# Instance norm over 512 channels: a small early write to the output, moved behind the first unit's sum

## The chip, the cores and the metric

The kernel runs on one core of a Trainium2 chip. The metric is the device time of one execution, in microseconds (us). A profile is one execution recorded by the hardware profiler; its span runs from the core's first to its last instruction. PE is TensorE, DVE is VectorE, ACT is ScalarE, POOL is GpSimd, SP is SyncE; ACTq, SPq and POOLq are the instruction queues from which DMAs are issued.

## What is computed

`x` has the shape (4, 8, 16, 256, 256) in float32, `gamma` the shape (8, 16). Each of the 4 x 8 x 16 = 512 channels is normalised over its own 256 x 256 = 65,536 values and scaled:

```
mu = x.mean(axis=(3, 4), keepdims=True)
var = ((x - mu) ** 2).mean(axis=(3, 4), keepdims=True)
out = (x - mu) / np.sqrt(var + 1e-5) * gamma[None, :, :, None, None]
```

134.2 MB are read and as many written.

## The kernel before

**Tiling.** The 512 channels are cut into 32 units of 16 channels. A unit is a tile of 128 partitions by 8,192 float32 values (4.19 MB, 4,096 KB in the profile): a channel lies on 8 neighbouring partitions. Six slots `xt` (AHEAD = 6) hold units in SBUF; unit u uses slot u mod 6. A unit is read once, changed in place and written back from its slot.

**One unit** (the loop over u, lines 103 to 134). VectorE sums each partition's row (L105); ScalarE sums the squares of the same row (L106, its elementwise result thrown away in `junk`); TensorE multiplies both sums with a small constant matrix, which adds the 8 partitions of a channel (L114); VectorE and ScalarE make the variance, the root, the reciprocal and the scale (L115, L119, L123, L125); VectorE applies shift and scale to the tile in place (L128). The store of the unit is issued from ScalarE's queue (L132), and the load of unit u + 6 into the same slot, which has to wait until that store has landed, from SP's queue (L48).

**Before the loop.** The loads of units 0 to 5 are issued at once, units 1 and 3 from ScalarE's queue, the others from SP's. GpSimd loads gamma into `g_row` (L55) and builds the constant matrix `navg` (L65 to L70); VectorE spreads gamma (`g_rep`, L81), TensorE turns it into a column (L86), VectorE copies that to `g_col` (L92), which L125 reads first for unit 0.

**The touch.** `touch` is a tile of 16 partitions by 128 float32 values. VectorE fills it with zeros (L53), and GpSimd's first DMA (L54) writes it to the first 512 bytes of every eighth row of unit 0 of `out`: 16 pieces of 512 bytes. Unit 0's store overwrites them later, so the result does not depend on them. Both write the same bytes, so the store of unit 0 waits on its queue until the touch has landed.

**What sets the order.** The kernel declares a manual schedule: every engine runs its instructions in the order in which the program names them. An engine's queue is strictly in order: an instruction that waits holds up all that stand behind it on that engine, issues of DMAs included. On ScalarE's queue the square of unit u + 1 stands behind the store of unit u. On GpSimd's queue nothing stands behind the building of `navg`.

Of the kernel before, what the change touches and what calls it, by code (L numbers as in the profile page):

```python
# [1 line left out]

# [4 lines left out]

F32 = mybir.dt.float32
U8 = mybir.dt.uint8
ALU = mybir.AluOpType  # L10
ACTF = mybir.ActivationFunctionType
AX = mybir.AxisListType


@with_exitstack
def kernel(
    ctx: ExitStack,
    tc: tile.TileContext,
    x: bass.AP,
    gamma: bass.AP,  # L20
    out: bass.AP,
):
    nc = tc.nc
    B, G, C, H, W = x.shape
    P = nc.NUM_PARTITIONS
    HW = H * W
    n_ch = B * G * C
    S = 8
    K = P // S
    F = HW // S  # L30
    U = n_ch // K
    NG = (G * C) // K
    AHEAD = 6
    assert HW % S == 0 and (G * C) % K == 0

    xv = x.rearrange("b g c h w -> (b g c h w)").rearrange("(u p f) -> u p f", p=P, f=F)
    ov = out.rearrange("b g c h w -> (b g c h w)").rearrange("(u p f) -> u p f", p=P, f=F)
    gv = gamma.rearrange("g c -> (g c)")

    data = ctx.enter_context(tc.tile_pool(name="data", bufs=1))  # L40
    singles = ctx.enter_context(tc.tile_pool(name="singles", bufs=1))
    psum = ctx.enter_context(tc.tile_pool(name="psum", bufs=4, space=bass.MemoryType.PSUM))
    ctx.enter_context(tc.manual_schedule())

    slots = [data.tile([P, F], F32, name=f"xt{i}") for i in range(AHEAD)]

    def load(u, queue):
        queue.dma_start(out=slots[u % AHEAD][:], in_=xv[u])  # L48


    g_row = singles.tile([1, G * C], F32, name="g_row")
    touch = singles.tile([16, 128], F32, name="touch")
    nc.vector.memset(touch[:], 0.0)  # L53
    nc.gpsimd.dma_start(out=ov[0][0::S, 0:128], in_=touch[:])  # L54
    nc.gpsimd.dma_start(out=g_row[:], in_=gv[None, :])  # L55
    for u in range(AHEAD):
        load(u, nc.scalar if u in (1, 3) else nc.sync)


    eps_t = singles.tile([P, 1], F32, name="eps_t")  # L60
    nc.gpsimd.memset(eps_t[:], 1e-5)
    one = singles.tile([1, 1], F32, name="one")
    nc.gpsimd.memset(one[:], 1.0)
    navg = singles.tile([P, K, S], F32, name="navg")
    nc.gpsimd.memset(navg[:], -1.0 / HW)  # L65
    nc.gpsimd.affine_select(  # L66
        out=navg[:], in_=navg[:], pattern=[[-S, K], [0, S]], compare_op=ALU.is_ge,
        fill=0.0, base=0, channel_multiplier=1,
    )
    nc.gpsimd.affine_select(  # L70
        out=navg[:], in_=navg[:], pattern=[[S, K], [0, S]], compare_op=ALU.is_ge,
        fill=0.0, base=S - 1, channel_multiplier=-1,
    )
    navg_w = navg[:].rearrange("p k s -> p (k s)")
    root_eps = singles.tile([P, 1], F32, name="root_eps")
    nc.scalar.activation(out=root_eps[:], in_=eps_t[:], func=ACTF.Sqrt)  # L76
    g_rep = singles.tile([1, NG, K, S], F32, name="g_rep")
    g_ps = psum.tile([P, NG], F32, name="g_ps", bufs=1)
    g_col = singles.tile([P, NG], F32, name="g_col")

    nc.vector.tensor_copy(  # L81
        out=g_rep[:],
        in_=g_row[:].rearrange("o (n k) -> o n k", n=NG).unsqueeze(3).to_broadcast([1, NG, K, S]),
    )
    for n in range(NG):
        nc.tensor.matmul(  # L86
            out=g_ps[:, n : n + 1],
            lhsT=g_rep[:, n].rearrange("o k s -> o (k s)"),
            rhs=one[:],
            start=True, stop=True,  # L90
        )
    nc.vector.tensor_copy(out=g_col[:], in_=g_ps[:])  # L92

    junk = singles.tile([P, F], U8, name="junk")

    st = singles.tile([P, U, 2], F32, name="st")
    nvar = singles.tile([P, U], F32, name="nvar")
    std = singles.tile([P, U], F32, name="std")
    rstd = singles.tile([P, U], F32, name="rstd")
    scale = singles.tile([P, U], F32, name="scale")  # L100

    squares = []
    for u in range(U):
        t = slots[u % AHEAD]
        nc.vector.reduce_sum(out=st[:, u, 0:1], in_=t[:], axis=AX.X)  # L105
        square = nc.scalar.activation(  # L106
            out=junk[:], in_=t[:], func=ACTF.Square, accum_out=st[:, u, 1:2],
        )
        if u:

            tc.declare_no_dep(square.ins, squares[-1].ins, reason="junk, ordered by the root between")
        squares.append(square)
        ps = psum.tile([P, 2], F32, name="ps")
        nc.tensor.matmul(out=ps[:], lhsT=navg_w, rhs=st[:, u], start=True, stop=True)  # L114
        nc.vector.tensor_scalar(  # L115
            out=nvar[:, u : u + 1], in0=ps[:, 0:1], scalar1=ps[:, 0:1],
            scalar2=ps[:, 1:2], op0=ALU.mult, op1=ALU.add,
        )
        nc.scalar.activation(  # L119
            out=std[:, u : u + 1], in_=nvar[:, u : u + 1], func=ACTF.Sqrt,  # L120
            bias=eps_t[:], scale=-1.0,
        )
        nc.vector.reciprocal(out=rstd[:, u : u + 1], in_=std[:, u : u + 1])  # L123
        g = u % NG
        nc.vector.tensor_mul(  # L125
            out=scale[:, u : u + 1], in0=rstd[:, u : u + 1], in1=g_col[:, g : g + 1],
        )
        nc.vector.tensor_scalar(  # L128
            out=t[:], in0=t[:], scalar1=ps[:, 0:1], scalar2=scale[:, u : u + 1],
            op0=ALU.add, op1=ALU.mult,  # L130
        )
        nc.scalar.dma_start(out=ov[u], in_=t[:])  # L132
        if u + AHEAD < U:
            load(u + AHEAD, nc.sync)


# [1 line left out]
_INS = ['x', 'gamma']  # L138
_OUTS = [((4, 8, 16, 256, 256), 'float32')]


# [23 lines left out]
```

## Time and profile before

| | before |
|---|---|
| median of 3 runs | 627.45 us (626.88 to 627.5) |
| span of the profiled execution | 625.4 us (its whole time is not listed) |
| busy: VectorE, ScalarE, PE, POOL | 443.4, 238.8, 21.4, 2.4 us |
| moved by DMA | 268.46 MB, 429 GB/s over the span |
| packets of queue q10 (issues of ACT) | 142.61 MB, 52.9% of the 16 DMA engines' span |
| packets of queue q1 (issues of SP) | 125.83 MB, 46.7% |
| packets of queue q0 (issues of POOL) | 0.01 MB, 0.0% |

Busy times are shares of the work of each engine and say little here by themselves. The page gives the DMA engines' rate in 40 equal slices of the span; the chain that ended last follows the last instruction back to what released it; a group's row gives the busy time, the mean duration and the idle time ahead of it with what ended it; a row of DMA issues gives the time from the issue to the landing; the table of stretches gives busy times and rates between two points of time, counted from the start of the span.

### The profile page before, as it was taken

To read this page: it belongs to the slowest core of one execution; us is meant where nothing else is said; L and a number is where in the kernel's file an instruction comes from. 1 tells how busy PE (TensorE), PEld (TensorE's weight loads), DVE (VectorE), ACT (ScalarE), POOL (GpSimd) and SP (SyncE) were. 2 spreads that over 40 slices of the span, in tenths; PEclk is the share of its full clock that TensorE was granted. 3 is DMA by queue.
4 is the path that set the end of the run, shared out by engine and by line. 5 is a ranking of instruction groups with operands and counts; after the bars stand their busy time and mean duration, and the time that the engine had idled before them with its cause. 6 is when DMAs were issued, how large, how long until landed. Compare 5 with 4: busy or idle time off the path is not lost.

```text
span 625.4 us, 631 instructions
## 1 busy us (share of the span) xinstructions
PE 21.4 (3%) x80; PEld 19.5 (3%) x80; DVE 443.4 (71%) x163; ACT 238.8 (38%) x98; POOL 2.4 (0%) x11
## 2 busy tenths in 40 slices
PE   0200000000000000000000000000000000000000
PEld 0200000000000000000000000000000000000000
DVE  0588999999776687666776767867668676686730
ACT  0444444444443244432344423444224442244400
POOL 1000000000000000000000000000000000000000
DMA  8999999999999999999999999999999999999998
GB/s 369 436 402 436 436 436 436 436 434 424 434 436 432 432 428 434 436 436 436 436 434 423 434 436 432 436 428 434 434 436 436 436 436 432 425 434 434 434 432 363
DMA packets 9282, 268.46 MB, mean 429 GB/s; under 512 B 1072, under 2 KB 1088, under 8 KB 1088
## 3 DMA queue, kind: packets, MB, share of 16 engines
q10 hardware_dynamic: 4896, 142.61, 52.9%
q1 hardware_dynamic: 4320, 125.83, 46.7%
q0 software_dynamic: 64, 0.01, 0.0%
q14 instruction: 2, 0.02, 0.0%
HBM read 134.22 MB, written 134.23 MB: 429 GB/s over the span
## 4 chain that ended last, share of the span: by engine, by line
another core or an unknown queue 61%; DMA 17%; DVE 15%; SPq 1%; PE 1%; issue 0%; ACT 0%
DVE st L105 10%; DMA xt<-in_x_dram 10%; DMA out_dram<-xt 8%; DVE xt L128 5%; SPq L48 1%; PE ps L114 1%; ACT std L119 0%; DVE nvar L115 0%; DVE rstd L123 0%; DVE scale L125 0%
## 5 line engine op out<-in xcount | busy, mean ns | idle before, releaser
L105 DVE TENSOR_REDUCE st<-xt 128x1 f32<-128x8192 f32 x32 | 277.9, 8685 | 100.8 <-DMA xt<-in_x_dram 100.8
L106 ACT ACTIVATE junk<-xt 128x8192 uint8<-128x8192 f32 x32 | 225.0, 7030 | 275.6 <-DMA xt<-in_x_dram 232.4
L128 DVE TENSOR_SCALAR xt<-xt,ps,scale 128x8192 f32<-128x8192 f32 x32 | 145.6, 4551 | 1.2
L119 ACT ACTIVATE std<-nvar,eps_t 128x1 f32<-128x1 f32 x32 | 9.4, 295 | 79.6 <-DVE nvar L115 79.6
L114 PE MATMUL ps<-st,navg 128*128 128x2 f32 x64 | 17.8, 348 | 557.6 <-DVE st L105 557.6
L114 PEld LDWEIGHTS ps<-st,navg 128*128 128x128 f32 x64 | 16.0, 311 | 559.4 <-issue 559.4
L115 DVE TENSOR_SCALAR nvar<-ps 128x1 f32<-128x1 f32 x32 | 9.2, 288 | 23.8 <-PE ps L114 23.8
L123 DVE RECIPROCAL rstd<-std 128x1 f32<-128x1 f32 x32 | 5.3, 164 | 11.6 <-ACT std L119 11.6
L81 DVE COPY g_rep<-g_row 1x1024 f32<-1x1024 f32 x1 | 0.7, 681 | 14.2 <-DMA g_row<-in_gamma_dram 14.2
L106 ACT ACTIVATION_READ_ACCUMULATOR junk<-xt 128x1 f32 x32 | 6.0, 187 | 0.0
L125 DVE TENSOR_TENSOR scale<-rstd,g_col 128x1 f32<-128x1 f32 x32 | 5.1, 160 | 1.1
L86 PE MATMUL g_ps<-one,g_rep 1*128 1x1 f32 x16 | 3.5, 347 | 16.1 <-DVE g_rep L81 16.1
L86 PEld LDWEIGHTS g_ps<-one,g_rep 1*128 1x128 f32 x16 | 3.5, 326 | 16.1 <-issue 16.1
L92 DVE COPY g_col<-g_ps 128x8 f32<-128x8 f32 x1 | 0.2, 167 | 3.7 <-PE g_ps L86 3.7
L76 ACT ACT_TABLE_LOAD x1 | 1.3, 1283 | 1.7 <-PEq L149 1.7
L53 DVE MEMSET touch<- 16x128 f32 x1 | 0.2, 165 | 0.9 <-PEq L149 0.9
L54 POOL DMA_DIRECT2D out_dram<-touch x1 | 0.6, 617 | 0.8 <-DVE touch L53 0.8
L55 POOL DMA_DIRECT2D g_row<-in_gamma_dram x1 | 0.5, 484 | 0.0
L66 POOL TENSOR_SCALAR_AFFINE_SELECT navg<-navg 128x128 f32<-128x128 f32 x1 | 0.4, 398 | 0.1
L70 POOL TENSOR_SCALAR_AFFINE_SELECT navg<-navg 128x128 f32<-128x128 f32 x1 | 0.4, 397 | 0.1
L65 POOL MEMSET navg<- 128x128 f32 x1 | 0.2, 231 | 0.0
L76 ACT ACTIVATE root_eps<-eps_t 128x1 f32<-128x1 f32 x1 | 0.2, 203 | 0.0
(6 smaller groups left out, 0.6 us busy)
## 6 DMA issues: line engine op xcount, KB each, us to landing
out_dram<-xt ACTq DMA_DIRECT2D x32, 4096.0 KB, 62.5
xt<-in_x_dram SPq DMA_DIRECT2D x30, 4096.0 KB, 38.5
xt<-in_x_dram ACTq DMA_DIRECT2D x2, 4096.0 KB, 31.7
out_dram<-touch POOLq DMA_DIRECT2D x1, 8.0 KB, 9.1
g_row<-in_gamma_dram POOLq DMA_DIRECT2D x1, 0.5 KB, 13.3
```

What stands on the lines that cost most here:

```text
L48: queue.dma_start(out=slots[u % AHEAD][:], in_=xv[u])
L76: nc.scalar.activation(out=root_eps[:], in_=eps_t[:], func=ACTF.Sqrt)
L81: nc.vector.tensor_copy(out=g_rep[:], in_=g_row[:].rearrange("o (n k) -> o n k", n=NG).unsqueeze(3).to_broadcast([1, NG, K, S]),)
L86: nc.tensor.matmul(out=g_ps[:, n : n + 1], lhsT=g_rep[:, n].rearrange("o k s -> o (k s)"), rhs=one[:], start=True, stop=True,)
L105: nc.vector.reduce_sum(out=st[:, u, 0:1], in_=t[:], axis=AX.X)
L106: square = nc.scalar.activation(out=junk[:], in_=t[:], func=ACTF.Square, accum_out=st[:, u, 1:2],)
L114: nc.tensor.matmul(out=ps[:], lhsT=navg_w, rhs=st[:, u], start=True, stop=True)
L115: nc.vector.tensor_scalar(out=nvar[:, u : u + 1], in0=ps[:, 0:1], scalar1=ps[:, 0:1], scalar2=ps[:, 1:2], op0=ALU.mult, op1=ALU.add,)
L119: nc.scalar.activation(out=std[:, u : u + 1], in_=nvar[:, u : u + 1], func=ACTF.Sqrt, bias=eps_t[:], scale=-1.0,)
L123: nc.vector.reciprocal(out=rstd[:, u : u + 1], in_=std[:, u : u + 1])
L125: nc.vector.tensor_mul(out=scale[:, u : u + 1], in0=rstd[:, u : u + 1], in1=g_col[:, g : g + 1],)
L128: nc.vector.tensor_scalar(out=t[:], in0=t[:], scalar1=ps[:, 0:1], scalar2=scale[:, u : u + 1], op0=ALU.add, op1=ALU.mult,)
```

## The change

The memset of `touch` and its DMA are no longer issued ahead of the gamma load but inside the loop, for unit 0 only, right after VectorE's first sum:

```diff
     g_row = singles.tile([1, G * C], F32, name="g_row")
     touch = singles.tile([16, 128], F32, name="touch")
-    nc.vector.memset(touch[:], 0.0)
-    nc.gpsimd.dma_start(out=ov[0][0::S, 0:128], in_=touch[:])
     nc.gpsimd.dma_start(out=g_row[:], in_=gv[None, :])
...
     for u in range(U):
         t = slots[u % AHEAD]
         nc.vector.reduce_sum(out=st[:, u, 0:1], in_=t[:], axis=AX.X)
+        if u == 0:
+
+            nc.vector.memset(touch[:], 0.0)
+            nc.gpsimd.dma_start(out=ov[0][0::S, 0:128], in_=touch[:])
         square = nc.scalar.activation(
```

The memset does not read the sum: it comes after it because VectorE runs in order. GpSimd's DMA waits for the memset. Its instruction now stands last on GpSimd's queue, behind the building of `navg`; the gamma load stands first there. The store of unit 0 waits for the touch as before.

## The prediction

> **What bounds the kernel now.** I read the bandwidth row of the page first, then the chain that ended last, then a table of stretches. In the page's row below each figure is the rate of one fortieth of the span (15.6 us).
>
> ```profile
> GB/s 369 436 402 436 436 436 436 436 434 424 434 436 432 432 428 434 436 436 436 436 434 423 434 436 432 436 428 434 434 436 436 436 436 432 425 434 434 434 432 363
> ```
>
> It is flat from the second slice to the thirty-ninth, whatever the engines do: VectorE is busy 71%, ScalarE 38%. Apart from its two ends only the third slice (31 to 47 us) is low, at 402. The chain of waits tells the same from the other side (start, duration, what):
>
> ```profile
> 112.28 0.02 issue
> 112.30 47.77 DMA out_dram<-xt
> ...
> 160.44 18.97 another core or an unknown queue
> ```
>
> Unit 5's store is issued at 112.3 and lands 47.8 us later, since other transfers stand ahead of it. From there each load waits in SP's queue for the store that frees its slot, about 19 us a time (the row says unknown queue; the waits of SP's own queue name the stores, 534.9 us in 26 waits). To see what a unit costs I took stretches of 19.36 us, the spacing of those waits. The columns are the stretch, its length, then PE, PEld, DVE, ACT and POOL busy, granted clock, DMA share, GB/s:
>
> ```profile
> 1.00:20.36 19.36, 3.54 (x16) 3.49 (x16) 0.90 (x3) 1.49 (x2) 2.18 (x7) 1.00 0.97 407
> 20.36:39.72 19.36, 0.56 (x2) 0.50 (x2) 15.97 (x6) 9.11 (x4) 0.00 (x0) 1.00 1.00 433
> 39.72:59.08 19.36, 0.56 (x2) 0.50 (x2) 18.18 (x6) 11.85 (x4) 0.00 (x0) 1.00 1.00 410
> 59.08:78.44 19.36, 1.12 (x4) 1.00 (x4) 17.01 (x10) 8.71 (x6) 0.00 (x0) 1.00 1.00 433
> ```
>
> Long stretches from 97.8 to 485 also give 433. One load and one store are 8.39 MB, and 8.39 MB at 433 GB/s is 19.37 us: **the transfers set the time**. 268.46 MB at 433 are 620.0 us of the 625.4. The stretch from 39.72, in which the first store starts, lost (433 - 410)/433 x 19.36 = 1.03 us, the first one (433 - 407)/433 x 19.36 = 1.16. So the change can cost only what makes the DMA engines idle or slow, and can gain little more than these two losses, 2.2 us.
>
> The span is 625.4 us; the profiled execution's whole time is not listed. The median 627.45 is 2.05 above the span, and I put my differences on the median.
>
> **The change, part by part.** The rows around the place where the touch goes (start, duration, engine, line, operation, idle time before it):
>
> ```profile
> 22.57 8.69 DVE L105 TENSOR_REDUCE st<-xt 128x1 f32<-128x8192 f32 x1 [2.71 <-DMA xt<-in_x_dram]
> ...
> 32.00 0.29 DVE L115 TENSOR_SCALAR nvar<-ps 128x1 f32<-128x1 f32 x1 [0.74 <-PE ps L114]
> ...
> 33.05 4.55 DVE L128 TENSOR_SCALAR xt<-xt,ps,scale 128x8192 f32<-128x8192 f32 x1
> ...
> 37.63 0.35 ACTq L132 DMA_DIRECT2D out_dram<-xt  x1
> 38.03 7.03 ACT L106 ACTIVATE junk<-xt 128x8192 uint8<-128x8192 f32 x1 [5.41 <-DVE xt L128]
> ```
>
> and the issues (KB each, us from issue to landing):
>
> ```profile
> out_dram<-touch POOLq DMA_DIRECT2D x1, 8.0 KB, 9.1
> g_row<-in_gamma_dram POOLq DMA_DIRECT2D x1, 0.5 KB, 13.3
> ```
>
> *Taken from the start.* One memset (L53, 0.165 us), POOL's 0.85 us wait for it and one issue (0.617 us). The gamma load, next on POOL's queue, starts at about 1.36 - 0.85 = 0.51 us instead of 1.98, and its row lands between 0.51 + 9.1 = 9.6 and 0.51 + 13.3 = 13.8 us, not at 15.29. g_rep, 16 small matmuls and g_col (done at 19.87) come earlier by as much. Their first reader is L125 at 32.85: 13 us of cover, worth nothing. SP and ACT issue their first loads at 0.81 as before. 8 KB less in the first stretch is 8192 B at 433 GB/s = 0.02 us. Gain 0.
>
> *The memset after the first sum.* L105 ends at 31.26; the memset takes 0.165 us in VectorE's idle 0.74 us before L115 (which waits for PE). Cost 0; without that cover, 0.165 us of VectorE.
>
> *POOL's issue.* It is now POOL's last instruction, so nothing stands behind it. Before, POOL began 0.30 us after the memset's end (1.06 to 1.36); now 31.43 + 0.30 = 31.73, ending at 32.35, ahead of L128. The landing time beside a busy VectorE and in midstream is not shown. Nearest row: its own, 9.1 us, with four loads queued then too; I take 40.8. Later by rows: g_row's 13.3 gives 45.0; if POOL's work were held until L128 ends at 37.60, 37.60 + 9.1 = 46.7; a load's 38.5 us (median), the far end, 70.2. Below nothing: alone in its queue it may land sooner, which gains nothing, because L128 ends at 37.60 anyway.
>
> VectorE's L128 sweeps its tile in 4.55 us, L105 one of the same size in 8.69. [...]
>
> *Store 0.* L132 on ACT's queue waits for the touch, since both write unit 0 of out: issued at 40.8 instead of 37.63. What does that cost? In ACT's queue stand loads 1 and 3 ahead of it. SP's and ACT's queues share evenly: loads 0 and 1 land 21.7 and 21.9 us after issue, 2 and 3, issued at 1.2, after 41.4 and 41.5, at 42.6. Store 0, issued at 37.63, lands after 24.9 us at 62.5, one period of 19.4 after that 42.6. So it lies idle for some 4 to 5 us now. An issue moves bytes within 1.2 us (issued at 0.81, 328 GB/s between 1.00 and 2.00): 40.8 + 1.2 = 42.0 is in time. Cost 0. If the touch is later, ACT's queue is empty, but SP's holds loads 4 and 5, due at 62.3 and 81.7, and they take the bandwidth. A lone queue of stores runs at 431 GB/s (596 to 616 us); a lone queue of loads no row shows. It lies between 433 and 339, the rate from 1 to 4 us, the start included.
>
> *Behind store 0 on ACT* is unit 1's square: 38.03 becomes 41.2, done with its accumulator read (0.19) at 48.4. PE waited for VectorE's sum at 46.2, now for this: unit 1 is 2.2 us late, and so are the units behind it up to unit 5, issued at 114.5. Its store had 47.8 us of other transfers ahead of it: cover enough. Store 1 (52.56 to 54.8) is still ahead of store 0's end. Cost 0.
>
> Sum: 0, **627.4 us**.
>
> **The rivals.**
> *B, the loss at the first store goes.* If the 1.03 us stands for a first write to out that the touch at 1.36 prepared too early, a touch just ahead cures it: 627.45 - 1.03 = 626.4. For it: no later store shows a dip of that size. Against: nothing shows that the touch works on it. With all of the start's loss too, 625.2.
> *C, a first write in midstream.* The touch went in while the first stretch was losing 1.16 us anyway; among full queues it may cost a loss of its own, as store 0 does: +1.03, 628.5; twice that (data, then completion), 629.5. Against: the stretch has ordinary reasons for its loss (no bytes before 1.00).
> *D, the touch is late (the slower side).* The mechanism: store 0 waits on ACT's queue for a touch that lands after about 41.4, and loads 4 and 5 alone keep the engines going. At 46.7 store 0 moves at 47.9, 5.3 us after 42.6; 5.3 x (1 - 339/433) = 1.15 us at most: 628.6. From 42.6 + 19.4 = 62.0 on, both queues are dry and each us costs one: a touch at 70.2 gives 71.4 - 62.0 = 9.4 us, 636.9. For it: every transfer of before beside full queues took 9 us or more. Against: 16 us lie between 46.7 and 62.
> *E, the change does not do what it says.* A scheduler could move the touch back; but the order is written by hand, and in the built kernel the memset stands right after sum 0 and the issue last on POOL: 2%.
>
> **How the numbers follow.** About 0.2% (1.25 us) is what a measurement of this kernel tells from no change. A, my forecast: 0.36, 627.2 to 627.7. B: 0.14, half over the bound. C: 0.22, 0.13 over it. D: 0.26, 0.24 over it, since a late touch would also bring C's loss into full queues (1.15 + 1.03 = 2.2). E: 0.02. Faster 0.07; slower 0.13 + 0.24 = 0.37; same 0.36 + 0.07 + 0.09 + 0.02 + 0.02 = 0.56. The range leaves out B's outer half (0.07) and D's long waits (about 0.10): 626.2 to 629.8 (627.45 + 2.2, rounded up).
>
> **What the profile after would show.** A: landing of the touch 9 to 10 us after an issue at 31.7, store 0's issue at about 40.8, the stretch from 39.72 at 410 again, 433 behind it. B: that stretch near 433. C: a second low stretch, around 36 to 41. D: POOL's issue longer than 0.62 us or a landing past 45, and less than 433 while SP's queue runs alone. I am wrong if the rate of the long middle changes, or the start before 2 us moves.

## The result and the profile after

The changed kernel takes **642.65 us** (median of 4 runs, 641.61 to 643.71) against 627.41 (median of 4, 626.88 to 627.5): a ratio of 1.0245, 95% interval 1.0232 to 1.0259. The prediction was 627.4 us with a range of 626.2 to 629.8. The change costs 15 us where I had counted nothing. The profiled execution has a span of 639.9 us and took 641.61. The granted clock is 1.00 in every run of this document.

I read the views in the same order as before. The bandwidth row of the changed kernel's page:

```profile
GB/s 381 438 394 434 434 406 428 418 434 422 426 426 422 422 428 424 430 430 426 432 426 418 428 420 434 426 426 426 430 426 426 428 422 430 420 424 436 430 434 213
```

Up to the fifth slice it looks as before. From the sixth (80 us) on, the plateau, 423 to 436 before, has gone down: 406 in the sixth, then 418 to 434, with 436 in one late slice; the last slice holds half a slice's bytes. The table of stretches, with the same columns as before (the last figure is GB/s), puts numbers on it:

```profile
1.00:20.36 19.36, 3.54 (x16) 3.48 (x16) 0.85 (x2) 1.49 (x2) 1.71 (x6) 1.00 0.97 406
20.36:39.72 19.36, 0.55 (x2) 0.50 (x2) 15.99 (x7) 7.42 (x3) 0.51 (x1) 1.00 1.01 434
39.72:59.08 19.36, 0.59 (x2) 0.50 (x2) 17.26 (x6) 12.51 (x4) 0.00 (x0) 1.00 1.00 408
59.08:78.44 19.36, 1.12 (x4) 1.00 (x4) 17.11 (x7) 9.74 (x6) 0.00 (x0) 1.00 1.00 428
...
97.80:291.40 193.60, 6.14 (x22) 5.51 (x22) 148.93 (x56) 81.58 (x33) 0.00 (x0) 1.00 1.00 425
291.40:485.00 193.60, 5.02 (x18) 4.50 (x18) 134.29 (x47) 72.88 (x28) 0.00 (x0) 1.00 1.00 427
...
620.00:639.90 19.90, 0.00 (x0) 0.00 (x0) 0.00 (x0) 0.00 (x0) 0.00 (x0) 1.00 0.60 257
```

The same two long stretches of the kernel before, and its last one:

```profile
97.80:291.40 193.60, 6.14 (x22) 5.52 (x22) 151.51 (x55) 81.54 (x33) 0.00 (x0) 1.00 1.00 433
291.40:485.00 193.60, 5.58 (x20) 5.01 (x20) 138.49 (x50) 74.19 (x30) 0.00 (x0) 1.00 1.00 433
...
616.00:625.40 9.40, 0.00 (x0) 0.00 (x0) 0.00 (x0) 0.00 (x0) 0.00 (x0) 1.00 0.73 314
```

The place where the touch goes in (20 to 40 us) is as fast as ever, and the stretch of the first store loses what it lost before (408 against 410). The loss lies in what follows. From 97.8 to 485 us, (433 - 425)/433 x 193.6 + (433 - 427)/433 x 193.6 = 6.3 us; from 59 to 98 us, at 428 twice, 0.4 us; from 485 to 580, at 426, 1.5 us. The tail of 19.9 us at 257 GB/s lacks (433 - 257)/433 x 19.9 = 8.1 us of full rate, before's tail 2.6: 5.5 us more. Together 13.7 of the 14.5 us by which the span grew. The DMA engines are called busy throughout (share 1.00) and move less.

The trace's packet records say how. A packet of 32,768 bytes takes 1.213 us of its engine (the median, before and after). Each engine moves 8 packets of a store and 8 of a load in a period, and before they take turns, one from ACT's queue, one from SP's (all 5,271 neighbouring pairs between 100 and 500 us). (The records do not name the engine; I put packets together by the end of one and the start of the next.) Between 60 and 580 us, 15 of 6,878 such packets took more than 1.26 us before, and 505 of 6,756 after, up to 2.2 us. Of the 505, 434 are loads, and about 300 of these stand in the two turns behind the end of a store on the same engine; in the first part, from 60 to 200 us, 135 of 140 do. Their excess is 8.7 us for each engine, close to the 8.2 us of the stretches. And the engines come apart: the first and the last engine's completion of one store lie 1.1 us apart before (unit 25), and 8.7 us after; in the tail the first engine has finished at 629.3 us and the last at 638.6.

The chain of waits has the same form, with a longer step: before, SP waited 18.97 us from load to load, now 19.0 to 20.1.

```profile
98.38 46.35 DMA out_dram<-xt
144.78 0.33 SPq L48
145.11 19.23 another core or an unknown queue
...
321.96 19.99 another core or an unknown queue
```

And the rows around the touch (start, duration, engine, line, operation, idle time before it), with the issues' rows:

```profile
31.33 0.17 DVE L106 MEMSET touch<- 16x128 f32 x1
...
31.80 0.51 POOL L107 DMA_DIRECT2D out_dram<-touch  x1 [28.63 <-DVE touch L106]
...
33.15 4.55 DVE L130 TENSOR_SCALAR xt<-xt,ps,scale 128x8192 f32<-128x8192 f32 x1
...
39.76 0.35 ACTq L134 DMA_DIRECT2D out_dram<-xt  x1
40.16 7.03 ACT L108 ACTIVATE junk<-xt 128x8192 uint8<-128x8192 f32 x1 [7.43 <-DMA out_dram<-touch]
...
62.30 0.56 PE L116 MATMUL ps<-st,navg 128*128 128x2 f32 x2 [14.38 <-DVE st L103]
```

```profile
g_row<-in_gamma_dram POOLq DMA_DIRECT2D x1, 0.5 KB, 9.2
out_dram<-touch POOLq DMA_DIRECT2D x1, 8.0 KB, 7.9
```

The memset hides behind PE, the touch is issued at 31.80 and lands at 31.80 + 7.88 = 39.68, and unit 0's store is issued at 39.76 in place of 37.63: 2.1 us late. By unit 2 PE waits for VectorE's sum again, at 62.30 where it did so at 61.27 before: the compute is 1.0 us late and gets no later. All of this is close to the prediction, and none of it explains 15 us by itself.

### The profile page after: what moved, and what is told of

Its sections match the earlier page's. It is cut to its first block, busy times and chain, and to the rows that moved or that the text cites. A ratio compares the mean times of both kernels' runs of the same rounds, so it can differ in the third digit from the quotient of the medians.

```text
span 639.9 us, 631 instructions
## 1 busy us (share of the span) xinstructions
PE 21.4 (3%) x80; PEld 19.5 (3%) x80; DVE 443.3 (69%) x163; ACT 238.8 (37%) x98; POOL 2.4 (0%) x11
## 4 chain that ended last, share of the span: by engine, by line
another core or an unknown queue 64%; DMA 14%; DVE 9%; issue 5%; ACT 1%; SPq 1%; PE 0%; POOL 0%; ACTq 0%; POOLq 0%
DMA out_dram<-xt 7%; DMA xt<-in_x_dram 6%; DVE st L103 5%; DVE xt L130 4%; DMA out_dram<-touch 1%; SPq L48 1%; ACT junk L108 1%; PE ps L116 0%; ACT std L121 0%; DVE nvar L117 0%; DVE rstd L125 0%; DVE scale L127 0%; POOL g_row L53 0%; POOL navg L64 0%
## 5 line engine op out<-in xcount | busy, mean ns | idle before, releaser
L130 DVE TENSOR_SCALAR xt<-xt,ps,scale 128x8192 f32<-128x8192 f32 x32 | 145.6, 4551 | 1.2
## 6 DMA issues: line engine op xcount, KB each, us to landing
xt<-in_x_dram SPq DMA_DIRECT2D x30, 4096.0 KB, 36.8
```

Of the source, the lines that this page charges most:

```text
L130: nc.vector.tensor_scalar(out=t[:], in0=t[:], scalar1=ps[:, 0:1], scalar2=scale[:, u : u + 1], op0=ALU.add, op1=ALU.mult,)
```

## The experiments

At first I had three theories. **P**: the late store misses its turn among the transfers, and from then on stores and loads end at different times, which costs. **T**: the small GpSimd write disturbs full queues. **W**: the first write to out is dear, and the touch must be early to make it cheap.

### Touch or lateness

*Late store, touch early.* The kernel before, with VectorE busy for 2.1 us ahead of unit 0's store; multiplying by 1.0 leaves the values as they are.

```diff
+        if u == 0:
+            nc.vector.tensor_scalar(
+                out=t[:, 0:3840], in0=t[:, 0:3840], scalar1=1.0, scalar2=None, op0=ALU.mult,
+            )
         nc.scalar.dma_start(out=ov[u], in_=t[:])
```

> The touch stays where it was before, as GpSimd's first action; unit 0's store alone is made late: VectorE multiplies 3840 of the tile's 8192 columns by 1.0 in place, about 2.1 us, so the store is issued near 39.8 us, as in the changed kernel, and not at 37.6. Theory P (step): what costs is that ACT's queue comes late to the DMA engines, misses a turn, and from then on the ends of stores and loads no longer fall together; each end outside the step stretches transfers and pulls the 16 engines apart. P expects about the changed kernel's time, 640 to 644 us, a rate of 425 to 428 GB/s from 98 to 485 us, and a long tail at a low rate. Theory T (the touch in midstream): the small GpSimd write among full queues disturbs the engines. T expects 627 to 628 us and 433 GB/s. Theory W (first write to out): T's number as well.

Measured: issue at 39.89, four runs of 643.29, 642.47, 644.24 and 633.74 us, 430 and 427 GB/s in the middle (in the profiled execution, the one of 643.29). Its store and its middle:

```profile
39.89 0.35 ACTq L136 DMA_DIRECT2D out_dram<-xt  x1
...
97.80:291.40 193.60, 6.15 (x22) 5.52 (x22) 150.78 (x56) 81.58 (x33) 0.00 (x0) 1.00 1.00 430
```

The lateness alone brings the loss, though not in the same amount each time: the four runs lie 6.9 to 17.4 us above the kernel before (median 626.86).

*Touch late, into another unit.*

```diff
-            nc.gpsimd.dma_start(out=ov[0][0::S, 0:128], in_=touch[:])
+            nc.gpsimd.dma_start(out=ov[5][0::S, 0:128], in_=touch[:])
```

> The touch at its new place, same size, same time (about 31.8 us), but into unit 5's rows of out, so that unit 5's store waits for it (it is issued past 110 us anyway) and unit 0's store does not. P expects the time of before, 627 to 628 us, unit 0's store issued near 37.7 us and 433 GB/s in the middle. T and W expect the changed kernel's 640 to 644 us, since the same small write goes into the same full queues.

Measured: 626.9 us, ratio 1.0001 (0.9991 to 1.001). Its stretch of the first store and its middle, and its touch and store:

```profile
39.72:59.08 19.36, 0.56 (x2) 0.50 (x2) 18.18 (x6) 11.85 (x4) 0.00 (x0) 1.00 0.99 406
97.80:291.40 193.60, 6.15 (x22) 5.52 (x22) 151.59 (x55) 81.59 (x33) 0.00 (x0) 1.00 1.00 433
```

```profile
31.83 0.51 POOL L107 DMA_DIRECT2D out_dram<-touch  x1 [28.66 <-DVE touch L106]
33.18 4.55 DVE L130 TENSOR_SCALAR xt<-xt,ps,scale 128x8192 f32<-128x8192 f32 x1
37.76 0.35 ACTq L134 DMA_DIRECT2D out_dram<-xt  x1
```

The same write at the same moment costs nothing once no early store waits for it. T falls.

*No touch* (its two lines and its tile taken out).

> No touch and no memset at all. P expects 627 to 628 us, as before: unit 0's store is issued near 37.7 us. W (the touch must come early because it makes the first write to out cheap) expects a time near the changed kernel's, or at least over 630 us, and a larger loss than 1.0 us in the stretch from 39.72 us. T expects 627 to 628 us.

Measured: 626.82 us, ratio 0.9999 (0.9989 to 1.0009); the stretch of the first store at 415. W falls: in this kernel the touch does nothing for the time, and the loss of about 1 us at the first store is there without it.

*The changed kernel, loads 4 and 5 held until store 0 is issued.*

```diff
-    for u in range(AHEAD):
+    for u in range(4):
         load(u, nc.scalar if u in (1, 3) else nc.sync)
...
         nc.scalar.dma_start(out=ov[u], in_=t[:])
+        if u == 0:
+            nc.scalar.activation(out=slots[4][:, 0:1], in_=eps_t[:], func=ACTF.Square)
+            load(4, nc.sync)
+            load(5, nc.sync)
```

> The changed kernel, touch at its new place and unit 0's store late, but SP's loads 4 and 5 are held until that store has been issued (ScalarE writes one column of slot 4 right behind the issue, and load 4 overwrites it). So both queues run dry near 41 us and start together. P expects the dry stretch as the only loss, 2 to 5 us, 629 to 633 us, and 432 to 434 GB/s in the middle. T and W expect the changed kernel's 640 to 644 us plus those 2 to 5 us.

Measured: 628.4 us (627.66 to 631.87), ratio 1.0027 (1.0013 to 1.004), 433 GB/s in the middle, with the touch late and the store issued at 39.71. The 15 us are gone. But the queues did not start in step, as I had meant them to: store 0 lands at 63.0, 3.0 us ahead of load 4 (66.0), and the later stores stay 3.6 to 4.2 us ahead of theirs. So what this run shows is that a late touch and a late store need not cost, and that stores about 3.7 us ahead of the loads beside them run at full rate.

### Is "in step" the right word?

Four kernels to see which distance costs; the distance is how much later a store lands than the load beside it, store 0 than load 4. Two of them vary the lateness as above (two passes over all 8,192 columns; one over 1,000).

> The touch first as before; unit 0's store made late by about 9.1 us (VectorE multiplies the whole tile by 1.0 in place, twice), so it is issued near 46.8 us, after ACT's queue has run dry. Theory P1 (any store that ends behind the load beside it costs): 636 to 645 us, whatever the distance. Theory P2 (only a short distance costs, where the end of a store falls next to the start of a load): near 627 to 630 us, since the queues are then about half a unit apart. Theory C (the prediction's: SP's queue takes the bandwidth over): 627 to 628 us.

Measured: issue at 46.52, 627.14 us, ratio 1.0 (0.9991 to 1.0009), 433 GB/s. **P as I had put it falls**: a store 9 us late, far out of step, costs nothing. While it is missing, loads alone move, at 437 GB/s from 42 to 48 us (390 from 42.6 to 51; the stretch from 39.72 to 59.08 has 406, before 410):

```profile
42.00:48.00 6.00, 0.00 (x0) 0.00 (x0) 5.97 (x3) 1.08 (x1) 0.00 (x0) 1.00 1.01 437
```

> The touch first; unit 0's store made late by about 0.55 us (1000 columns multiplied by 1.0), so issued near 38.2 us. ACT's queue reaches it in before at about 43 us, and in the changed kernel a store issued at 39.76 moved its first bytes at about 44.0, 4.3 us after the issue. By that lead a store issued at 38.2 is ready at 42.5, still in time: P1 and P2 expect 626.5 to 628 us. If the margin is smaller than that, 636 to 645 us.

Measured: issue at 38.29, 626.67 to 631.35 us in ten runs, median 628.58, ratio 1.0027 (1.0008 to 1.0046). Against the median of 627.17 beside it, five runs lose at most 0.4 us and five lose 2.4 to 4.2: neither of the two expectations.

*Stores ahead.* The changed kernel, where loads 4, 5 and 6 are named behind unit 1's square.

```diff
+        if u == 1:
+            nc.scalar.activation(out=slots[4][:, 0:1], in_=eps_t[:], func=ACTF.Square)
+            load(4, nc.sync)
+            load(5, nc.sync)
+            load(6, nc.sync)
...
-        if u + AHEAD < U:
+        if u and u + AHEAD < U:
```

> The changed kernel, with loads 4 and 5 held longer: until ScalarE has done unit 1's square, about 47.4 us (load 6 is named behind them, as it would otherwise stand in front of them on SP's queue). The stores then run 4 to 8 us ahead of the loads beside them. P with direction (a store that ends behind the load costs, one that ends ahead of it does not): 432 to 434 GB/s in the middle and 626 to 630 us. P without direction (any distance between the two ends costs): 425 to 430 GB/s in the middle, 636 to 645 us.

Measured: 628.31 us, ratio 1.0018 (1.0009 to 1.0028), 433 GB/s in the middle. The stores run further ahead than expected: store 0 lands 17.2 us ahead of load 4, and from unit 10 on a store lands 11.3 us ahead of its load. Loads land every 19.4 us, so that is also 8.1 us behind the load in front: the run shows one more distance without a cost, and decides nothing about 4 to 8 us ahead.

*Half stores.*

```diff
-        nc.scalar.dma_start(out=ov[u], in_=t[:])
+        nc.scalar.dma_start(out=ov[u][0 : P // 2], in_=t[0 : P // 2])
+        nc.scalar.dma_start(out=ov[u][P // 2 : P], in_=t[P // 2 : P])
```

> The kernel before with each store issued as two DMAs of 64 partitions, so that a store ends in the middle of each load as well. If the end of a store in the middle of a load is what costs, 427 GB/s or less in the middle and 636 us or more. If the end of a store costs nothing as long as the units' ends stay together, 627 to 629 us and 433 GB/s.

Measured: four runs of 701.53 to 729.87 us against 627.17, 381 and 390 GB/s in the middle. This is no clean test of the end of a store. Here stores are stretched as much as loads (between 60 and 580 us 714 packets of stores and 715 of loads took more than 1.26 us), unlike in the changed kernel, so halving the partitions probably does something of its own. What that is stays open: no run here separates it from the end of a store.

### How wide the bad place is

The same edit as in the first experiment with 1,980, 2,880, 4,860, 5,940, 8,192 and twice 6,120 columns.

> The touch first; unit 0's store late by about 1.1 us (1980 columns multiplied by 1.0 in place), issued near 38.8 us. With the 4.3 us lead it is ready at 43.1, just past its turn at 43.0. Theory N (near miss: a store that ends one turn or so behind the load beside it costs, a larger distance doesn't): between 629 and 644 us, because some engines miss the turn and some don't. Theory G (cost grows or falls smoothly with lateness): half of the 15 us, near 634 us, in every run.

> Late by about 3.3 us (5940 columns), issued near 41.0 us: SP's queue gets about two packets ahead. N: a cost still, but less than at 2.1 us, 628 to 640 us. G: 636 to 642 us (falling from 642.9 at 2.1 us to 627.1 at 9.1 us).

> Late by about 4.6 us (8192 columns), issued near 42.2 us. N: 627 to 629 us and 433 GB/s in the middle. G: 636 to 640 us.

> Late by about 6.8 us (6120 columns, twice), issued near 44.4 us. N: 627 to 629 us and 433 GB/s in the middle. G: 630 to 634 us.

> The kernel before with unit 0's store late by about 1.6 us (2880 columns), issued near 39.3 us; a point of the curve between 1.1 us (629.8) and 2.1 us (642.9). If the cost depends on all engines missing the same turn, near 640 us; if on how many miss it, between 630 and 642 us.

> Late by about 2.7 us (4860 columns), issued near 40.4 us; a point between 2.1 us (642.9) and 3.3 us (627.2). A narrow position: 627 to 632 us; a broad one: 635 to 643 us.

The table holds these and the ones above. Issue, distance and rate are those of the one profiled execution of each kernel, which need not be typical where the times scatter: for 3,840 columns it is the run of 643.3, for 4,860 the one of 641.7, for 8,192 the one of 632.2 us. The distance is the landing of store 0 less that of load 4, both from the trace's issues and landings; before it is 62.5 - 62.3 = 0.2 us, in the changed kernel 65.3 - 60.9 = 4.4.

| kernel | store 0 issued | distance | GB/s, 98 to 291 and 291 to 485 | time of the runs |
|---|---|---|---|---|
| before | 37.63 | 0.2 | 433, 433 | 626.7 to 627.7 |
| 1,000 columns | 38.29 | 0.2 | 433, 433 | 626.7 to 631.4 |
| 1,980 | 38.91 | 1.2 | 433, 433 | 629.0 to 631.3 |
| 2,880 | 39.47 | 4.5 | 426, 424 | 642.5, 643.3, 674.3, 674.6 |
| the change | 39.76 | 4.4 | 425, 427 | 641.6 to 643.7 |
| 3,840 | 39.89 | 3.7 | 430, 427 | 633.7, 642.5, 643.3, 644.2 |
| 4,860 | 40.43 | 3.8 | 429, 429 | 630.9, 631.4, 632.5, 641.7 |
| 5,940 | 41.02 | 6.9 | 433, 433 | 627.0 to 627.6 |
| 8,192 | 42.22 | 8.5 | 433, 433 | 626.9 to 628.6, once 632.2 |
| 2 x 6,120 | 44.49 | 12.1 | 433, 433 | 626.9 to 627.2 |
| 2 x 8,192 | 46.52 | 16.9 | 433, 433 | 627.0 to 627.6 |

Theory N (a near miss) holds in the main, and G, a cost that grows or falls smoothly, falls. N missed at 5,940 columns, where it still expected a cost: the place is narrower. The points that lose rate in the middle are issued between 39.47 and 40.43, their neighbours that don't at 38.91 and 41.02, so the bad place is between 1.0 and 2.1 us wide in the time of issue; the change's 39.76 lies in it. In it the times scatter most. Two runs with 2,880 columns took 674 us, more than either expectation and 31 us more than the change; neither was profiled, and I can't explain them. With 4,860 columns three runs lie in the narrow expectation or 0.5 us over it, and one in the broad one. Ratios outside the bad place: 1.0048 (1.0032 to 1.0063) for 1,980 columns, 1.0004 (0.9995 to 1.0013) for 5,940, 1.0015 (0.9999 to 1.0031) for 8,192 and 0.9999 (0.9989 to 1.0009) for 2 x 6,120. Where 1,980 columns and the single run of 632.2 us lose, the middle is at 433 and the engines end apart instead: their completions of unit 25's store lie 3.9 and 5.5 us apart. In the bad place the runs of one kernel scatter too far for one ratio, so the table lists all of them.

### The issue of the loads, or the distance

SP issues a load when the store ahead of it has landed (in the changed kernel load 6 at 65.31, with store 0's landing at 65.3), and a later store moves that issue too. Three kernels take the two apart. GpSimd fills part of the freed slot first, and SP's load waits for that; the load overwrites the fill.

```diff
         if u + AHEAD < U:
+            nc.gpsimd.memset(t[:, 0:2048], 0.0)
             load(u + AHEAD, nc.sync)
```

> The kernel before, but each load in the loop is issued later: GpSimd first fills 2048 columns of the freed slot (after the store has landed), and SP's load waits for that, about 2 us. Stores and loads still start in step. Theory I (the issue: what stretches transfers is a load that SP issues while the running load is in its second or third round, as in the changed kernel): 632 to 645 us and under 430 GB/s in the middle. Theory L (the distance itself, a store one turn behind its load): 627 to 628 us and 433 GB/s.

Measured: 628.09 us, ratio 1.0013 (1.0003 to 1.0022), 433 GB/s; a fill takes 1.80 us.

> The changed kernel, with each load of the loop issued later in the same way, 5120 columns, about 5 us. The store is one turn behind its load as in the changed kernel, but the issue falls later into the running load. I: 627 to 631 us. L: 638 to 645 us.

Measured: 643.7 us (642.84 to 644.68), ratio 1.0265 (1.025 to 1.0281), distance 65.4 - 61.0 = 4.4 us, 425 GB/s twice. The fill took 4.36 us, 7.20 the first time, and the loads' landing fell from 36.8 to 32.4 us: the issue did move.

> The kernel before with the hold of 5120 columns, about 5 us: the control for the two others. I: 627 to 629 us, since the issue falls past the third round. L: 627 to 629 us. Above 632 us, the hold itself costs and the two others say nothing.

Measured: 627.99 us, ratio 1.0013 (1.0003 to 1.0022). By the traces SP issues load 6 at 4.4 us behind the landing of load 4 in the changed kernel, at 2.1 with the fill of 2,048 columns, at 4.7 here and at 11.8 (7.6 to 8.6 for later loads) in the changed kernel with the hold. So this kernel issues its loads close to the changed kernel's place and keeps 433 GB/s, and the changed kernel issues them far from it and keeps the loss: I falls, and L, the distance, stands.

### The changed kernel, made later

> The changed kernel with unit 0's store made later still: VectorE multiplies 5940 columns of the tile by 1.0 in place (3.3 us) ahead of the store, so it is issued near 41.1 us in place of 39.8. If the position of the first store, and not the touch, makes the 15 us, more delay takes them away: 627 to 629 us and 433 GB/s in the middle (a kernel with 1.3 us more of waiting, 15 us faster). If the touch in midstream is part of it, 635 us or more.

The edit is that of the first experiment with 5,940 columns, made in the changed kernel. Measured: **626.98 us** (626.78 to 627.65), ratio 1.0003 (0.9993 to 1.0012). Its touch, its store and its stretches:

```profile
31.76 0.51 POOL L107 DMA_DIRECT2D out_dram<-touch  x1 [28.58 <-DVE touch L106]
33.11 4.55 DVE L130 TENSOR_SCALAR xt<-xt,ps,scale 128x8192 f32<-128x8192 f32 x1
40.98 0.35 ACTq L138 DMA_DIRECT2D out_dram<-xt  x1
```

```profile
39.72:59.08 19.36, 0.56 (x2) 0.50 (x2) 18.18 (x7) 10.19 (x4) 0.00 (x0) 1.00 1.00 411
...
97.80:291.40 193.60, 6.14 (x22) 5.51 (x22) 154.76 (x56) 81.59 (x33) 0.00 (x0) 1.00 1.00 433
291.40:485.00 193.60, 5.58 (x20) 5.01 (x20) 138.50 (x50) 74.17 (x30) 0.00 (x0) 1.00 1.00 433
```

The touch stands where the change put it, the store is issued 1.2 us later than in the changed kernel, and the kernel is 15.7 us faster. The row to look at is the 433 behind 97.8. No version here beats the kernel before by more than a measurement can tell.

## Why the prediction was wrong, point by point

**What bounds the kernel** was right: the transfers. So was the sentence that the prediction would be wrong if the rate of the long middle changed, which is what happened.

**The parts at the start, the memset and POOL's issue** held in what they cost. One reading was off: POOL issued the gamma load at 1.32, not at 0.51, so the wait ahead of POOL's first issue was not the memset's. It landed 9.2 us after its issue (bounds 9.1 to 13.3), early enough either way. The touch was issued at 31.80 (31.73 predicted) and landed after 7.9 us (9.1). No run shows POOL's work held until VectorE's sweep of the tile ends, the source of the 46.7 us in the sum for D: here the issue ended at 32.31, ahead of L130 at 33.15, and by the packet records the touch's bytes moved at 36.3 to 36.8, before L130's end at 37.7.

**Store 0** is the step that failed: its term, put at 0, is the 15.2 us. It failed in two places. First, "An issue moves bytes within 1.2 us ... 40.8 + 1.2 = 42.0 is in time." The 1.2 us came from the very start, with empty queues. Behind full ones the packet records show 4.8 us from the issue at 39.76 to the first engine's first bytes at 44.5, and 6.9 us on the last engine; the two latest stores (2 x 6,120 and 2 x 8,192 columns), whose own queue had run dry while SP's was full, took 4.8 to 5.1 and 5.4 to 5.9 us. (In the expectations above I had read 4.3 us for the first.) Where loads 4 and 5 were held, so that SP's queue was not full, the same store moved its first bytes 1.4 to 1.9 us after its issue. What the prediction took for 4 to 5 us of idle time before store 0 was mostly this lead: before, its first bytes move at 43.3, 5.7 us after the issue. So store 0 was not in time at 39.76, and at 37.63 it had little to spare: 0.7 us more already cost half of the runs 2.4 us and more.

Second, and worth the 15 us: "Cost 0. If the touch is later, ACT's queue is empty, but SP's holds loads 4 and 5, due at 62.3 and 81.7, and they take the bandwidth." For the moment itself that is true: a store 9 us late costs nothing, and in that run the lone queue of loads moved 437 GB/s from 42 to 48 us and 390 from 42.6 to 51. What I left out is that the queues remember. Where store 0 starts beside load 4 sets the distance between the ends of the later stores and loads: before it is 0.2 us for every unit up to 26, and in the changed kernel made later 6.7 at the start and 6.0 to 6.2 from unit 5 to 26. (That nothing in the loop waits for both would explain it; this is argued and not tested.) In the changed kernel that distance is 4.4 us at the start, the place at which load packets are stretched when a store ends, unit after unit, and then the engines drift apart and the distance shrinks to between 2.4 and 3.4 us (units 10 to 26). I had looked for a cost at the place of the change and not for a state that the change leaves behind.

**The cover of unit 1's late square** held: 39.76 against 40.8 for the store, 40.16 against 41.2 for the square, and PE waits for VectorE again at unit 2, 1.0 us late where 2.2 were predicted.

**The rivals.** B (the 1.03 us at the first store vanish) fell: that stretch is at 410 GB/s with the touch early, 406 and 408 with it late, 415 without it. C (a first write in midstream) fell with the touch into unit 5, 434 GB/s from 20.36 to 39.72 us and no loss. D had the right event, store 0 late through a late touch, and the right sign. Its mechanism and its point of decision were wrong: it wanted a touch past 41.4 us and a rate lost while SP's queue ran alone, with more lateness costing more. The touch came before that, the lone queue cost nothing, and more lateness cures the loss. E fell.

**What stays open.** Shown is that the position of the first store makes the cost, without the touch, and that neither the issue of the loads nor a later or smaller distance does. Why stores that land 3.7 to 4.5 us behind their loads stretch packets, and those 0.2 or 6.7 us behind or 3.7 us ahead do not, is not settled, nor why the times in the bad place scatter. The spread between the engines is no cause by itself: in the kernel made later, the engines' first bytes of store 0 are spread over 2.3 us, as in the changed one (2.1), and the spread of its completions is 2.3 us and stays so up to unit 25 (changed kernel: 8.7 there). Whether HBM, SBUF or the engine's own order of reads and writes is behind it I could not tell with the records at hand.

## What to carry to other kernels

Here two streams of equal size keep the DMA engines full, and a delay of one early transfer was not paid once: it set how the streams lie against each other for the rest of the run, so that a wait of 2 us cost 15 us and a longer one nothing. Expect this where a kernel is built the same way; other sizes and rates were not tried. Read the rate of the long middle first; if it has moved while the work is the same, look at the distance between the landings of the two streams, and make the transfer later and earlier by a us or two before blaming the instruction that was moved. A small transfer that a large store waits for is best put where that store can't be late, or taken out: here the kernel without the touch took as long as the kernel before (ratio 0.9999).

## What the runs showed of the hardware

- Store 0's first bytes move 4.8 to 6.9 us after its issue in the changed kernel, where SP's queue is full, and 1.4 to 1.9 us after it where that queue is held empty.
- Full-rate transfer here is very regular: 1.213 us for each packet of 32,768 bytes, with 15 exceptions over 1.26 us in 6,878 before. A plateau of 425 in place of 433 GB/s is therefore a finding, not noise.
- Where store 0 lands 3.7 to 4.5 us behind load 4, the middle loses 1 to 2% of the rate; 0.2, 1.2 and 6.7 us or more behind lose nothing there, nor does a store 3.0 to 4.2 us ahead.
- Splitting each store into two of 64 partitions took the rate from 433 to between 381 and 390 GB/s and the time to over 700 us.
